# GpSimd subtracts the low parts of a weight tile in two instructions: a decoder trunk in emulated fp32

## The chip, the cores and the metric

The kernel runs on one core of a Trainium2 chip. The metric is the device time of one execution in microseconds (us); the number that counts is the median of the runs. One more execution was recorded by the hardware profiler, and all rows below are from that one.

## The reference

The program is a decoder trunk of two layers over 512 positions of width 1024, in float32, with a batch of one. In each layer the input is normalized, scaled and shifted by vectors that are computed from a condition vector (the "ada" vectors); one wide projection then gives everything that the two branches need:

```python
def hybrid_layer(x, mod, norm_g, w_in, ...):
    shift, scale, gate = jnp.split(mod, 3, axis=-1)
    h = rms_norm(x, norm_g) * (1 + scale[:, None]) + shift[:, None]
    a_qkv, a_z, m_cq, m_ckv, m_kr, m_z, merge = jnp.split(h @ w_in, SPLIT_IDX, axis=-1)
    y_a = dilated_mixer(a_qkv, rel_bias) * jax.nn.silu(a_z)
    y_m = mla_mixer(m_cq, m_ckv, m_kr, q_norm_g, w_uq, kv_norm_g, w_ukv, cos, sin) * jax.nn.silu(m_z)
    g_a, g_m = jnp.split(jax.nn.sigmoid(merge), 2, axis=-1)
    merged = g_a * (y_a @ w_out_a) + g_m * (y_m @ w_out_b)
    return x + gate[:, None] * (merged @ w_o)
```

Branch A is attention over dilated windows, with 3 groups of 8 heads and a bias by relative position; branch B is latent attention with 16 heads and a rotary part. A last normalization follows layer two.

## The kernel before

**Numbers in two parts.** Products are made in a format with a shorter mantissa (fp32r), and each operand is kept as a high part, its value rounded to that format, and a low part, the value less the high part. A product is the sum of three: high by high, low by high, high by low. `split` (line 195) makes the two parts. The high part is a copy on ACT (line 203) or a cast on DVE or POOL (line 205); the low part is one subtraction (line 206), on POOL unless `lo` names DVE. A table, `ENG`, gives for each use the engine of the high and of the low part in turn. POOL is the engine called GpSimd as well.

**Weights.** `wload` (line 231) brings a tile of weights of 1024 inputs by 128 outputs: `load_w` issues its DMA on SP's queue into a `stage` tile (line 224; two buffers), `wpair` takes a high tile `wh` and a low tile `wl` (three buffers each), and `split` fills them. In such a tile the 1024 inputs lie as 8 groups of 128 partitions, so the tile is 128 partitions by 8 x 128 values, 128x1024. The DMA that fills a stage tile again waits for its last reader, the subtraction. `proj` (line 248) then runs over the 8 groups: for each group k it issues three matmuls (line 166), `wh[k]` by the high part of the normalized input (`hTh`), `wl[k]` by the same, and `wh[k]` by the low part (`hTl`). The result lies in a PSUM bank; there are two banks `pj`, three `s`, two `t` and one `o`.

**Stages.** In each layer the projections come in blocks between attention steps: queries and keys of a set of heads (`a_qk`), values (`a_v`), SiLU gates (`zgate`, line 604, whose tile is evacuated at lines 609 and 610), merge gates (`merge_gate`), the latents of branch B (`m_latents`, whose second evacuation is line 952), then 16 heads of branch B (`m_head`), the output projections and the norm. An attention of branch A (`a_attn`) scales its weights `p` by factors of 128x8 values (lines 821 to 844 make them, line 854 scales, partly on DVE, partly on POOL, partly on ACT), transposes them (line 861), splits them into `pth` (line 211) and `ptl` (line 864), and multiplies them by the values `v` into the bank `o`. In layer 0 the ada vectors of later use are accumulated on DVE between these steps (line 286, after a first step on ACT at line 277; their weights are loaded into `lat` tiles at line 272, the sums added to their biases at line 306), the tables of position bias are written to memory and read back as `bvec` and `btile` (lines 529, 537, 541), and the angles of the rotary part are reduced on DVE in a chain of some 25 steps (lines 553 to 576).

**The order.** The program says what depends on what. In which order each engine and each DMA queue does its instructions is decided when the program is built: a scheduler with a simulated timeline (`schedule_with_timeline_sim=True`, line 1362) takes at each point what its estimates of duration say will be ready. An engine then does its list strictly in that order and waits wherever an operand isn't there. So when an instruction changes its count or its estimated length, other engines' lists can change as well.

## Time and profile before

| | us |
|---|---|
| median of 3 runs | 1435.63 |
| fastest and slowest of them | 1433.96, 1441.8 |
| the profiled execution, its own time | 1440.56 |
| its span in the trace | 1438.8 |
| PE busy | 1352.0 |
| DVE busy | 917.5 |
| ACT busy | 704.7 |
| POOL busy | 575.4 |

PE is the matrix engine, PEld its loading of weights beside it, DVE the vector engine, ACT the scalar engine, POOL GpSimd, SP the engine whose queue issues all DMAs. Line numbers are those of the kernel before. The trace gives each instruction's start and duration, and for idle time ahead of it what ended that idle time. The granted clock is the share of PE's full clock in a stretch: 1.00 is the higher of its two levels (2.4 GHz), 0.50 the lower (1.2 GHz).

### The profile page before, as it was taken

The page shows a single profiled execution, that of the slowest core. Times are in us where ns is not written, and L with a number is a line of the kernel's source. Part 1 is how long each engine was busy: PE and PEld are TensorE (multiplying, and loading weights), DVE is VectorE, ACT ScalarE, POOL GpSimd, SP SyncE. Part 2 cuts the span into 40 slices and gives each one's busy share as a digit, 9 for nine tenths or more (in the row PEclk, how much of TensorE's full clock was granted, in tenths as well). Part 3 has the DMA queues.
Part 4 walks back from the last instruction along what each step waited for, and adds up shares of the span by engine and source line. Part 5 has one row for each costly group of instructions (what it writes and reads, how often), then busy time and mean ns, then how long its engine had stood idle before and what let it go on. Part 6 is the DMA issues. An engine that isn't in the chain of part 4 may idle for free.

```text
span 1438.8 us, 21364 instructions
## 1 busy us (share of the span) xinstructions
PE 1352.0 (94%) x7351; PEld 1163.1 (81%) x7351; DVE 917.5 (64%) x2123; ACT 704.7 (49%) x1913; POOL 575.4 (40%) x423
## 2 busy tenths in 40 slices
PE   7989997999999999999989999999999898999997
PEld 6788776798887778888888988789888777888876
DVE  7736758845756767654799346634575586766563
ACT  4424663236566778721034266523655687862102
POOL 2423434334553333355444234533455333344530
PEclk7999998999999999999999999999999999999999
DMA  9776423233244323465753332233324332445641
GB/s 334 236 228 190 148 71 98 85 88 85 70 132 124 93 81 107 122 192 162 209 157 124 112 88 74 81 89 89 83 73 133 110 92 81 111 145 170 185 130 59
DMA packets 236676, 181.47 MB, mean 126 GB/s; under 512 B 16410, under 2 KB 204224, under 8 KB 236568
## 3 DMA queue, kind: packets, MB, share of 16 engines
q1 hardware_dynamic: 236568, 180.11, 42.3%
q8 instruction: 58, 0.95, 0.3%
q14 instruction: 50, 0.41, 0.1%
HBM read 150.60 MB, written 23.17 MB: 121 GB/s over the span
## 4 chain that ended last, share of the span: by engine, by line
PE 64%; DVE 15%; DMA 7%; ACT 5%; issue 5%; POOL 3%; SPq 1%; DVEq 0%; POOLq 0%; ACTq 0%
PE pj L166 38%; PE s L166 19%; PE o L166 4%; PE t L861 3%; DMA stage<-in_w_o 2%; POOL wl L206 2%; DMA lat<-in_w_ada 1%; DVE lat L286 1%; DMA stage<-in_w_in 1%; ACT mn L807 1%; DMA v<-in_w_ada 1%; DVE p L792 1%; DVE ptl L864 1%; DVE wh L205 1%; ACT p L798 1%
## 5 line engine op out<-in xcount | busy, mean ns | idle before, releaser
L206 POOL TENSOR_TENSOR wl<-stage,wh 128x1024 fp32r<-128x1024 f32 (+1 forms) x134 | 316.1, 2360 | 429.3 <-ACT wh L203 230.0
L166 PE MATMUL pj<-hTh,wh 128*128 128x512 f32 (+1 forms) x720 | 286.2, 398 | 22.4 <-DVE wh L205 5.7
L166 PE MATMUL pj<-hTl,wh 128*128 128x512 f32 (+1 forms) x720 | 281.2, 392 | 0.0
L166 PE MATMUL pj<-hTh,wl 128*128 128x512 f32 (+1 forms) x704 | 275.3, 391 | 0.0
L166 PEld LDWEIGHTS pj<-hTh,wh 128*128 128x128 f32 x720 | 138.3, 192 | 52.1 <-issue 14.1
L166 PEld LDWEIGHTS pj<-hTl,wh 128*128 128x128 f32 x720 | 137.0, 191 | 26.6 <-ACT hTl L377 0.7
L203 ACT ACTIVATE wh<-stage 128x1024 fp32r<-128x1024 f32 (+1 forms) x84 | 85.1, 1014 | 142.7 <-PE s L166 71.4
L166 PEld LDWEIGHTS pj<-hTh,wl 128*128 128x128 f32 x704 | 134.1, 191 | 23.4
L864 DVE TENSOR_TENSOR ptl<-t,pth 128x512 fp32r<-128x512 f32 (+2 forms) x160 | 96.4, 617 | 35.3 <-ACT pth L211 34.3
L211 ACT ACTIVATE pth<-t 128x512 fp32r<-128x512 f32 (+2 forms) x160 | 81.8, 537 | 65.4 <-PE t L861 63.5
L166 PE MATMUL s<-kb,qh 128*128 128x256 f32 (+3 forms) x384 | 86.4, 320 | 8.4 <-DVE x L792 3.3
L166 PE MATMUL o<-pth,v 128*64 128x128 f32 (+3 forms) x496 | 91.2, 260 | 3.0 <-DVE yy L915 1.7
L166 PE MATMUL o<-ptl,v 128*64 128x128 f32 (+2 forms) x320 | 79.9, 282 | 7.8 <-DVE ptl L864 7.7
L861 PE MATMUL t<-eye_r,p 128*128 128x128 f32 x560 | 83.9, 280 | 1.7 <-POOL p L854 1.6
L205 DVE CAST wh<-stage 128x1024 fp32r<-128x1024 f32 (+1 forms) x77 | 57.9, 753 | 40.6 <-PE s L166 16.0
L166 PEld LDWEIGHTS s<-kb,qh 128*128 128x128 f32 x384 | 66.5, 191 | 21.3 <-ACT qh L211 4.6
L1093 DVE CUSTOM_DVE_ANT_0 p<-s,cs 128x512 f32<-128x512 f32 (+3 forms) x128 | 58.6, 484 | 30.9 <-PE s L166 30.4
L166 PEld LDWEIGHTS o<-pth,v 128*64 128x64 f32 (+1 forms) x496 | 65.5, 155 | 9.0 <-ACT pth L211 3.1
L861 PEld LDWEIGHTS t<-eye_r,p 128*128 128x128 f32 x560 | 65.6, 143 | 6.7 <-POOL p L854 2.0
L166 PE MATMUL s<-hTh,wh 128*128 128x512 f32 (+1 forms) x168 | 65.8, 392 | 2.3 <-DVE x L792 1.2
L166 PE MATMUL s<-hTh,wl 128*128 128x512 f32 (+1 forms) x168 | 65.5, 390 | 0.0
L166 PEld LDWEIGHTS o<-ptl,v 128*128 128x128 f32 (+1 forms) x320 | 52.4, 164 | 16.1 <-DVE ptl L864 11.8
(713 smaller groups left out, 3302.1 us busy)
## 6 DMA issues: line engine op xcount, KB each, us to landing
stage<-in_w_in SPq DMA_DIRECT2D x118, 512.0 KB
lat<-in_w_ada SPq DMA_DIRECT2D x64, 256.0 KB
v<-in_w_ada SPq DMA_DIRECT2D x32, 256.0 KB
stage<-in_w_in SPq DMA_DIRECT2D x32, 256.0 KB
gd<-gt SPq DMA_DIRECT2D x32, 256.0 KB
stage<-in_w_out_b SPq DMA_DIRECT2D x16, 512.0 KB
stage<-in_w_o SPq DMA_DIRECT2D x16, 512.0 KB
p<-yd SPq DMA_DIRECT2D x24, 256.0 KB
```

The lines of the kernel that those rows point to most:

```text
L166: T.matmul(o, l, r, start=start, stop=stop, skip_group_check=True)
L203: A.activation(dst_h, src, AF.Copy)
L205: hi.tensor_copy(dst_h, src)
L206: (lo or G).tensor_tensor(dst_l, src, f32(dst_h), ALU.subtract)
L211: A.activation(dst, src, AF.Copy)
L286: V.scalar_tensor_tensor(acc, st, cact[:, k:k + 1], side if k == ne + np_ else acc, ALU.mult, ALU.add)
L792: V.tensor_tensor_reduce(pt[e][:, sl], o[:, c0:c0 + 128], bts[e][:, 128 + 128 * g:256 + 128 * g], 1.0, -3e38, ALU.add, ALU.max, x12[:, e, ...
L798: A.activation(pt[e][:, sl], pt[e][:, sl], AF.Exp, bias=m12[:, g - 1, e, p:p + 1], scale=SA, accum_out=l12[:, g - 1, e, p:p + 1])
L807: (A.copy if c == "A" else (G if c == "G" else V).tensor_copy)(dst[32 * p:32 * p + 32, :, qb], src[32 * qb:32 * qb + 32, :, p])
L861: T.transpose(tp[:, 128 * b:128 * b + 128], s, eye)
L864: V.tensor_tensor(lo[:, :n], tp[:, :n], f32(h[:, :n]), ALU.subtract)
L1093: V.tensor_tensor_reduce(pt, o, mask[:, 512 - n:512], 1.0, -3e38, ALU.add, ALU.max, m[:, qb:qb + 1])
```

## The change

In `split`, if the low part is POOL's, and the tile has three dimensions with more than one group of inputs and 1024 values in a partition, POOL does the subtraction in two instructions, one for the first four groups of inputs and one for the last four:

```diff
--- before.py
+++ after.py
@@ -203,6 +203,12 @@
             A.activation(dst_h, src, AF.Copy)
         else:
             hi.tensor_copy(dst_h, src)
+        if lo is None or lo is G:
+            n = dst_l.shape[1]
+            if len(dst_l.shape) == 3 and n > 1 and n * dst_l.shape[2] == 1024:
+                for i in (0, n // 2):
+                    G.tensor_tensor(dst_l[:, i:i + n // 2], src[:, i:i + n // 2], f32(dst_h[:, i:i + n // 2]), ALU.subtract)
+                return
         (lo or G).tensor_tensor(dst_l, src, f32(dst_h), ALU.subtract)
 
     def hi_copy(dst, src, use):
```

That is so for 118 of the 126 subtractions of 128x1024 that POOL has; the other eight, the values of `a_v`, lie in four dimensions and stay whole. Nothing else is written differently. Behind line 207 the line numbers of the changed kernel are 6 higher.

The lists of the engines differ in places. The matmuls of PE are 6958 rows before, and 6622 of them stand in the same order in both; of 2062 rows of DVE 1965 do, of 1172 of ACT 1103, of 628 of SP 594. The differences lie in the first 100 us of layer 0, in layer 0 from the second attention of branch A to the latents, and at the end of both layers (the last heads and the merge gates). In the rows below a name has two numbers, of which the second differs between the two programs without meaning.

PE, layer 0, where the projection of keys (`s_478`) ends and the two tiles of a SiLU gate begin (`pj_489` with `wh_487` and `wl_488`; `pj_494` with `wh_492` and `wl_493`), before:

```order
L861 MATMUL t_422_2047<-eye_r_69,p_390_1859 128x128
L861 MATMUL t_422_2047<-eye_r_69,p_391_1860 128x128 x2
L166 MATMUL s_478_2395<-hTh_55_224,wl_477_2392 128x512
L166 MATMUL s_478_2395<-hTl_56_225,wh_476_2391 128x512
L166 MATMUL pj_489_2469<-hTh_41_210,wh_487_2465 128x512
L166 MATMUL pj_494_2503<-hTh_41_210,wh_492_2499 128x512
L166 MATMUL o_418_2029<-pth_420_2039,v_173_774 128x256
L166 MATMUL o_418_2029<-ptl_421_2040,v_173_774 128x256
L166 MATMUL o_418_2029<-pth_420_2039,v_175_802 128x256
L166 MATMUL o_418_2029<-ptl_421_2040,v_175_802 128x256
```

and now:

```order
L166 MATMUL s_478_2414<-hTh_55_224,wh_476_2409 128x512
L166 MATMUL s_478_2414<-hTh_55_224,wl_477_2410 128x512
L166 MATMUL s_478_2414<-hTl_56_225,wh_476_2409 128x512
L166 MATMUL pj_489_2489<-hTh_41_210,wh_487_2484 128x512
L166 MATMUL pj_494_2524<-hTh_41_210,wh_492_2519 128x512
L166 MATMUL pj_489_2489<-hTh_41_210,wl_488_2485 128x512
L166 MATMUL pj_489_2489<-hTl_42_211,wh_487_2484 128x512
L166 MATMUL pj_489_2489<-hTh_43_212,wh_487_2484 128x512
L166 MATMUL pj_489_2489<-hTh_43_212,wl_488_2485 128x512
L166 MATMUL pj_489_2489<-hTl_44_213,wh_487_2484 128x512
```

The seven transposes (`t_419`, `t_422`) ahead of the end of `s_478` have left, and the first products of the attention (`o_418` with `pth_420` and `ptl_421`) no longer follow the first matmuls of `pj_489` and `pj_494`: nearly all 48 matmuls of the two gate tiles come first, then the transposes, then a matmul of the next tile and `o_418`.

DVE, the same place, around its cast of `wh_492` (line 205), before:

```order
L213 CAST kb_117_453<-s_468_2325 64x4x128
L286 SCALAR_TENSOR_TENSOR lat_369_1818<-lat_374_1831,cact_75,lat_369_1818 128x512
L854 TENSOR_SCALAR p_398_1901<-p_398_1901,f12_417_2026 128x128 x3
L854 TENSOR_SCALAR p_399_1902<-p_399_1902,f12_417_2026 128x128
L428 SCALAR_TENSOR_TENSOR Ac_115_451<-Ac_115_451,vec_76 128x2
L854 TENSOR_SCALAR p_399_1902<-p_399_1902,f12_417_2026 128x128 x2
L667 TENSOR_TENSOR ql_474_2386<-pj_472_2360,qh_473_2385 128x512
L659 TENSOR_TENSOR kb_118_456<-s_468_2325,kb_117_453 64x4x128
L205 CAST wh_492_2499<-stage_491_2497 128x1024
L286 SCALAR_TENSOR_TENSOR lat_369_1818<-lat_375_1834,cact_75,lat_369_1818 128x512
```

and now:

```order
L840 TENSOR_TENSOR L_413_2013<-L_413_2013 128x8
L292 SCALAR_TENSOR_TENSOR lat_369_1831<-lat_374_1844,cact_75,lat_369_1831 128x512
L673 TENSOR_TENSOR ql_474_2404<-pj_472_2378,qh_473_2403 128x512
L665 TENSOR_TENSOR kb_118_459<-s_468_2342,kb_117_456 64x4x128
L841 RECIPROCAL L_413_2013<-L_413_2013 128x8
L205 CAST wh_492_2519<-stage_491_2517 128x1024
L312 TENSOR_TENSOR Bc_116_455<-ada_322_1564,vec_76 128x2
L312 TENSOR_TENSOR Ac_115_454<-ada_322_1564,vec_76 128x2
L292 SCALAR_TENSOR_TENSOR lat_369_1831<-lat_375_1847,cact_75,lat_369_1831 128x512
L843 TENSOR_TENSOR fn_414_2018<-en_412_2009,L_413_2013 128x8
L847 TENSOR_TENSOR f0_416_2037<-en_412_2009,L_413_2013 128x8
L434 SCALAR_TENSOR_TENSOR Ac_115_454<-Ac_115_454,vec_76 128x2
```

The scalings of `p` (line 854, now 860) stand behind the cast, as does the making of the factors `fn` and `f0`; the accumulations of an ada vector (`lat_369`), the evacuations of keys (`kb_118`) and the query's low part (`ql_474`) stand ahead of it as they did.

SP's queue, in the first 100 us of layer 0, where the position bias is written (`bvec`, `btile`) and weights of `a_v` are loaded (`stage_169` to `stage_187`), and two ada weights (`lat_208`, `lat_209`), before:

```order
L224 DMA stage_166_737<-in_w_in 128x4x256
L224 DMA stage_169_743<-in_w_in 128x4x256
L732 DMA stage_184_865<-in_w_in 128x2x256 x2
L529 DMA bvec_437<-gt_149_683 24x512
L732 DMA stage_187_896<-in_w_in 128x2x256 x2
L529 DMA bvec_437<-gt_152_691 24x384
L537 DMA btile_438<-bvec_437 8x32x256 x4
L541 DMA btile_438<-bvec_437 1024x1x128 x2
L272 DMA lat_208_1025<-in_w_ada 128x512
L272 DMA lat_209_1028<-in_w_ada 128x512
```

and now:

```order
L230 DMA stage_166_741<-in_w_in 128x4x256
L535 DMA bvec_440<-gt_149_687 24x512
L543 DMA btile_441<-bvec_440 8x32x256 x4
L230 DMA stage_169_748<-in_w_in 128x4x256
L738 DMA stage_184_870<-in_w_in 128x2x256
L535 DMA bvec_440<-gt_152_695 24x384
L738 DMA stage_184_870<-in_w_in 128x2x256
L547 DMA btile_441<-bvec_440 1024x1x128 x2
L278 DMA lat_208_1030<-in_w_ada 128x512
L738 DMA stage_187_901<-in_w_in 128x2x256 x2
L278 DMA lat_209_1033<-in_w_ada 128x512
```

The first write to `bvec` and the four to `btile` (line 537, now 543) stand ahead of `stage_169` and `stage_184`, and `lat_208` ahead of `stage_187`.

## Rows read from the trace of the kernel before

**Rows 1.** The page of the profiled execution: its line of busy times by engine, and from the chain of work that ended last the shares by engine and by line.

```profile
PE 1352.0 (94%) x7351; PEld 1163.1 (81%) x7351; DVE 917.5 (64%) x2123; ACT 704.7 (49%) x1913; POOL 575.4 (40%) x423
...
PE 64%; DVE 15%; DMA 7%; ACT 5%; issue 5%; POOL 3%; SPq 1%; DVEq 0%; POOLq 0%; ACTq 0%
PE pj L166 38%; PE s L166 19%; PE o L166 4%; PE t L861 3%; DMA stage<-in_w_o 2%; POOL wl L206 2%; DMA lat<-in_w_ada 1%; DVE lat L286 1%; DMA stage<-in_w_in 1%; ACT mn L807 1%; DMA v<-in_w_ada 1%; DVE p L792 1%; DVE ptl L864 1%; DVE wh L205 1%; ACT p L798 1%
```

**Rows 2.** Groups of POOL instructions by line and form (busy us, mean ns of one | idle time of POOL before them and what ended it): the weight subtraction at full size, another subtraction of half the size on the same line, and the eight weight subtractions that were of half the size already.

```profile
L206 POOL TENSOR_TENSOR wl<-stage,wh 128x1024 fp32r<-128x1024 f32 x126 | 305.8, 2428 | 414.8 <-ACT wh L203 215.6 <-DVE wh L205 133.3 <-issue 23.0
...
L206 POOL TENSOR_TENSOR pl<-p,ph 128x512 fp32r<-128x512 f32 x20 | 25.4, 1288 | 20.0 <-ACT ph L203 17.9 <-issue 1.9
...
L206 POOL TENSOR_TENSOR wl<-stage,wh 128x512 fp32r<-128x512 f32 x8 | 10.3, 1290 | 14.5 <-ACT wh L203 14.5
```

**Rows 3.** Waits of PE's weight loads by what ended them (us in total, times, longest us): the only row of the answer that names a weight subtraction of POOL.

```profile
PEld s L166 <- POOL wl L206: 0.6, 1, 0.6
```

**Rows 4.** The chain that ended last, in order of time (start us, us, what): the first and the last of the nine pieces that are a weight subtraction of POOL, and the load behind the first.

```profile
414.23 2.38 POOL wl L206
...
416.62 4.24 DMA stage<-in_w_in
...
1370.96 2.73 POOL wl L206
```

**Rows 5.** Waits of PE's matmuls by what ended them (us in total, times, longest us).

```profile
PE o L166 <- DVE ptl L864: 7.7, 12, 3.3
PE pj L166 <- DVE v L707: 6.6, 3, 4.9
PE pj L166 <- DVE wh L205: 5.7, 1, 5.7
```

**Rows 6.** Busy time by stretch of the span (stretch, its length, then for PE, PEld, DVE, ACT and POOL the busy us and the count of instructions, the granted clock of PE as a share of full speed, the DMA share, GB/s).

```profile
92.00:98.00 6.00, 6.00 (x16) 4.82 (x16) 3.31 (x5) 1.19 (x2) 2.36 (x1) 0.54 0.95 321
220.00:300.00 80.00, 67.83 (x370) 57.12 (x369) 61.50 (x97) 26.36 (x56) 33.66 (x27) 0.89 0.32 88
226.00:232.00 6.00, 0.45 (x2) 0.01 (x1) 5.88 (x13) 2.37 (x6) 5.43 (x6) 0.88 0.19 43
232.00:242.00 10.00, 6.26 (x36) 5.47 (x37) 9.53 (x14) 1.82 (x3) 2.73 (x1) 0.56 0.41 105
282.00:290.00 8.00, 7.52 (x24) 6.11 (x25) 3.76 (x7) 5.49 (x9) 0.00 (x0) 0.59 0.10 24
555.00:625.00 70.00, 67.37 (x367) 57.02 (x366) 49.56 (x118) 48.54 (x127) 25.20 (x17) 1.00 0.49 147
900.00:980.00 80.00, 77.94 (x452) 66.43 (x451) 40.40 (x84) 32.02 (x89) 37.37 (x31) 0.98 0.30 85
1235.00:1305.00 70.00, 68.06 (x370) 57.48 (x370) 48.53 (x116) 48.27 (x126) 24.43 (x16) 1.00 0.47 143
```

**Rows 7.** Timeline of PE (start us, us, instruction, in brackets the idle time before it and what ended it): two matmuls 0.23 us apart before the stop, the two that end it, the one after the next long stop, and the one that ends the stop at 91.65.

```profile
225.82 0.40 PE L166 MATMUL s<-hTl,wh 128*128 128x512 f32 x1
226.05 0.40 PE L166 MATMUL pj<-hTh,wh 128*128 128x512 f32 x1
232.12 0.77 PE L166 MATMUL pj<-hTh,wh 128*128 128x512 f32 x1 [5.67 <-DVE wh L205]
...
236.44 0.58 PE L166 MATMUL o<-ptl,v 128*128 128x256 f32 x1 [3.33 <-DVE ptl L864]
...
282.48 0.77 PE L166 MATMUL pj<-hTh,wh 128*128 128x512 f32 x1 [2.88 <-DVE lat L952]
...
91.65 0.81 PE L166 MATMUL pj<-wh,hTh 128*128 128x512 f32 x1 [4.93 <-DVE v L707]
```

**Rows 8.** Busy time of the scalings of line 854 alone in one stretch (columns as in the group above on stretches).

```profile
221.00:230.00 9.00, 4.11 (x12) 5.96 (x8) 1.00 0.55 146
```

**Rows 9.** Timeline of DVE around these stops.

```profile
216.67 2.38 DVE L832 TENSOR_TENSOR L<-l,en 128x8 f32<-128x8 f32 x1
...
230.21 1.77 DVE L205 CAST wh<-stage 128x1024 fp32r<-128x1024 f32 x1
...
232.56 2.30 DVE L306 TENSOR_TENSOR Bc<-ada,vec 128x2 f32<-128x2 f32 x1
...
281.59 0.74 DVE L952 SCALAR_TENSOR_TENSOR lat<-pj,vec,lat 128x512 fp32r<-128x512 f32 x1
```

**Rows 10.** Timeline of POOL in the same stretch.

```profile
216.59 2.43 POOL L206 TENSOR_TENSOR wl<-stage,wh 128x1024 fp32r<-128x1024 f32 x1 [0.48 <-ACT en L830]
...
232.11 2.73 POOL L206 TENSOR_TENSOR wl<-stage,wh 128x1024 fp32r<-128x1024 f32 x1 [0.68 <-issue]
```

**Rows 11.** The chain that ended last, from 76 us on (SPq is the queue of DMA issues on SP).

```profile
76.66 5.18 SPq L541
...
81.89 7.84 DMA lat<-in_w_ada
...
89.75 0.73 ACT lat L277
...
91.18 0.43 DVE v L707
```

## The prediction

> **What bounds the kernel now.** I began with the page's line of busy times and the chain that ended last. PE is busy 1352.0 of 1438.8 us, POOL 575.4, and the chain is PE for 64% and POOL for 3% [rows 1]: only about 87 us of the span are idle PE, and POOL has room. Then the groups of POOL by form: 126 weight subtractions of 128x1024 take 2428 ns each, and both forms of half that size on the same line take 1288 to 1290 ns [rows 2]. Then I asked who waits for them. PE's weight loads waited for a POOL weight subtraction once, for 0.6 us [rows 3]; PE's long waits are for DVE: 5.7 us for one cast of a high part, 7.7 for low parts of attention weights, 6.6 for low parts of V [rows 5]. In the chain a POOL subtraction stands nine times, between 414.23 and 1370.96 us, and there it holds a stage tile: behind the first, the next weight load of 4.24 us begins [rows 4]. Last I looked at where PE loses its time, by stretches. From 220 to 300 us PE is busy 67.83 of 80 us at a granted clock of 0.89; the stretch 680 us later, where layer 1 does the same stages, has 77.94 of 80 at 0.98 [rows 6]. So the largest loss lies at one place of layer 0, and DVE is what is full there: 5.88 of 6 us and 9.53 of 10.
>
> **The direct effect of the halves.** Two halves take 2 x 1.290 = 2.580 us where one took 2.428, so 0.152 us more. Of the 126 subtractions 118 are cut, which is 118 x 0.152 = 18 us more of POOL; POOL's 863 us of idle time cover it. A low part's first half is there 1.14 us sooner, its last half 0.15 us later. The sooner half is worth 0 to 0.6 us, since only 0.6 us of PE's waiting is for such a tile [rows 3]; I take 0, as PE comes to the first low block only after other work. The later end counts where the subtraction is in the chain: 9 x 0.152 = **+1.4 us**. If a DMA behind it were not waiting for the stage tile, this would be 0.
>
> **What the new order does.** The order of each engine is decided from a simulated timeline, so the longer POOL work shifts other instructions. I compared the orders: most of each list is kept, and three places are rewritten.
>
> First place, 220 to 300 us. PE stops at the first matmul of the second SiLU gate tile (wh_492) for 5.67 us, and then for 3.33 us at the first product with a ptl tile [rows 7]. DVE made the cast at 230.21, behind the scalings of line 854, which took it 4.11 us [rows 8, 9]. In the new order the cast stands ahead of all those scalings and of some small steps (about 1.5 us, an estimate from some ten instructions of 0.15 us), and POOL's subtractions for both gate tiles stand ahead of POOL's scalings. An 8-element DVE step that began at 216.67 beside a POOL subtraction lasted 2.38 us, until that subtraction ended [rows 9, 10]; with a half there it can be held 1.3 us at most, 1.1 less. So the cast begins 4.1 + 1.1 + 0.5 to 1.5 = 5.7 to 6.7 us sooner, at 223.5 to 224.5, and ends at 224.2 to 226.3, by whether it takes 0.7 or 1.77. PE needs it at 226.05, or 0.7 sooner, since seven transposes have left their place ahead of it. The stop of 5.67 becomes 0 to 0.9; I take 0.4. Ahead of the first ptl product PE now has 47 more matmuls of the two gate tiles at 0.227 each, 10.7 us. DVE has 14 to 16 us to do between the cast and that ptl (estimate: the 4.11 of scalings, the 3.7 that lay between the two before, and five to six us of evacuations and casts now ahead of it). So 3 to 5 us of a stop remain; I take 3.5 for the 3.33 of before. DVE stays the fuller engine, and the work that hides the gate tiles is not new work, only placed sooner.
>
> The third stop of this stretch, 2.88 us at 282.48, waits for line 952, which DVE did at 281.59 at the end of the long chain that makes the rope's angles [rows 7, 9]. The new order puts line 952 in the middle of that chain, but the chain begins later, since two attention pieces now come ahead. By the instructions in between I get stops of 0.5 and 2.5 where there was one of 2.88: nothing won.
>
> Each stop also costs clock. After the stops PE had 0.56 of its clock from 232 to 242 and 0.59 from 282 to 290, and did 6.26 and 7.52 us of work in them [rows 6]: 0.44 x 6.26 = 2.8 and 0.41 x 7.52 = 3.1 us lost, one of the two clock levels being half the other. I expect about the same loss again behind two or three short stops. The sum of the stretch: 5.67 + 3.33 + 2.88 = 11.9 before, 0.4 + 3.5 + 3.0 = 6.9 after, and the clock between 0 and 3 better: **-6.5 us**. Its bounds: all idle time gone (12.2) with both losses of clock (5.9) is -18; with nothing gained and two more slow stretches of 3 it is +6.
>
> Second place, the start of layer 0. PE stops for 4.93 us until 91.65 [rows 7]. The chain there: SP is held 5.18 us at line 541, then a load of 7.84 us, ACT's line 277 at 89.75, DVE's line 707 at 91.18 [rows 11]. In the new order the bias writes of lines 529 and 537 stand ahead of two weight loads, and one of the two later loads stands behind; line 541 is held for less. I estimate the load 3 to 6 us sooner, so the stop at 0 to 2, and up to 0.46 x 6 = 2.8 us of clock that PE lost from 92 to 98 [rows 6]. DMA moved 321 GB/s then at 0.95 of its time, so a part is given back to the next loads. I take **-3.0**, with bounds 0 and -7.7.
>
> Third place, the ends of both layers (head pieces and merge gates, 555 to 625 and 1235 to 1305 us). PE is busy 67.37 and 68.06 of 70 there at full clock [rows 6]: 4.6 us could be won at most, and a new order can open stops. I take **+1.0**, bounds -3 and +6.
>
> Elsewhere DVE steps that are held by a POOL subtraction are held shorter, as one of two elements that took 2.30 us beside a subtraction [rows 9, 10]; most of them lie off the chain: **-1.0**, bounds 0 and -5. What the row shows is stated as a rule by the Trainium skill, SBUF — State Buffer (Who interferes with whom): DVE and GpSimd share a pair of ports that one of them holds for its whole instruction while the other is blocked. By that rule alone, the cut would let DVE in halfway each time, and this term would be nearer to its far bound.
>
> The sum: 1.4 - 6.5 - 3.0 + 1.0 - 1.0 = -8.1, so 1440.56 becomes 1432.5. The median of the runs is 1435.63, 4.93 below the profiled execution; the same change puts it at **1427.5 us**.
>
> **Rivals.** *Only the halves act.* The stops at the first place move but keep their size, because DVE has the same work to do (15.4 us busy of the 16 from 226 to 242 [rows 6]); the second place gives back what it wins. Then +1.4 and at most -3 stay: about 1435. For it: DVE is full, and no instruction of DVE is removed. Against: 4.1 us of work is moved behind the cast that ends the longest stop.
>
> *DVE is freed by more than the order.* If the holds of DVE by POOL are halved wherever they stand in the chain, both long stops vanish and the clock stays up: -12 at the first place, -6 at the second, -1 elsewhere, +1.4: about 1418. For it: the DVE steps that began at 216.67 and 232.56 and the POOL subtraction beside each end together [rows 9, 10]. Against: the second half can follow the first at once, and hold DVE again. This is what the rule of the page named above would make of the time.
>
> *Slower.* The long stops turn into more stops. At the first place wh_492, the first ptl, and the two tiles of line 952 each stop PE; if the cast ends after 228 us and each stop is 2.5 to 3 us with 2.9 us of slow clock behind it, the place costs 4 x 5.7 = 22.8 in place of 11.9 + 5.9 = 17.8: +5. With +1.4 and a few us at the ends of the layers it gives about 1444. It decides from a cast that ends after 228.
>
> **How the numbers follow.** About 0.5% (7.2 us) is what a measurement here can tell from no change: faster is below 1428.4, slower above 1442.8. Chances: the forecast (1422 to 1433) 0.46, only the halves 0.25, DVE freed 0.14, slower 0.15. Of the forecast's some 0.30 lies below 1428.4 and 0.16 above; with the freed DVE and a little of the second that makes 0.46 faster; 0.41 same; 0.13 slower. The range 1414 to 1442 leaves out a part of the freest case and most of the slower one.
>
> **What would show it.** Right: POOL near 593 us; 118 pairs of 1.29; the matmul of wh_492 without a long stop and one of about 3.5 us at the first ptl; 220 to 300 us with PE busy 72 or more; the stop near 90 us under 2. Wrong: a cast of wh_492 after 228; new stops at the ends of the layers; pairs that take well over 2.6 us; PE waiting for a POOL weight tile.

## The result, and the profile after

| | before | after |
|---|---|---|
| median of the runs taken side by side, us | 1438.72 (4 runs, 1433.96 to 1441.93) | 1414.65 (4 runs, 1409.67 to 1415.47) |
| the profiled execution, its span, us | 1438.8 | 1407.6 |

The ratio is 0.9838, with a 95% interval of 0.9811 to 0.9865: 1.6% faster. The forecast of 1427.5 against 1435.63 was a ratio of 0.9943. The time lies inside the range, but the gain is nearly three times the forecast's.

The page of the kernel after, its busy times and the chain that ended last:

```profile
PE 1341.5 (95%) x7351; PEld 1156.2 (82%) x7351; DVE 903.9 (64%) x2123; ACT 703.3 (50%) x1913; POOL 598.4 (43%) x541
...
PE 70%; DVE 14%; ACT 5%; DMA 5%; issue 3%; POOL 1%; SPq 1%; DVEq 0%; ACTq 0%; POOLq 0%
```

Against [rows 1] the span fell by 31.2 us: PE's busy time by 10.5 and its idle time, span less busy, by 20.7 (86.8 to 66.1). That is more than the 24.1 us between the medians: the profiled execution of after is the fastest of its four (1409.67 us), that of before was slower than its median (1440.56). PE does the same 7351 matmuls, so less busy time means a higher clock. POOL grew by 23.0 us, and DVE, with the same 2123 instructions, fell by 13.6.

Groups of POOL by form, after (as [rows 2]):

```profile
L210 POOL TENSOR_TENSOR wl<-stage,wh 128x512 fp32r<-128x512 f32 x236 | 308.6, 1330 | 332.8 <-ACT wh L203 159.7 <-DVE wh L205 118.9 <-issue 31.4
L212 POOL TENSOR_TENSOR wl<-stage,wh 128x1024 fp32r<-128x1024 f32 x8 | 20.4, 2549 | 50.7 <-ACT wh L203 50.7
```

The 118 subtractions are 236 halves of 1330 ns. Next, stretches of PE: first before, then after, columns as in [rows 6] but of PE alone.

```profile
0.00:70.00 70.00, 60.27 (x256) 0.83 0.87 293
70.00:110.00 40.00, 35.07 (x186) 0.91 0.67 211
205.00:300.00 95.00, 82.83 (x456) 0.91 0.32 91
620.00:960.00 340.00, 328.49 (x1847) 0.98 0.43 126
960.00:1300.00 340.00, 326.76 (x1814) 1.00 0.37 103
```

```profile
0.00:70.00 70.00, 60.49 (x270) 0.88 0.91 304
70.00:110.00 40.00, 38.08 (x209) 1.00 0.73 221
205.00:300.00 95.00, 90.11 (x496) 1.00 0.38 104
620.00:960.00 340.00, 332.78 (x1923) 0.99 0.42 123
960.00:1300.00 340.00, 327.27 (x1773) 1.00 0.39 112
```

Read each row for two losses: its length less PE busy, and the busy time by which the clock fell short. In the 95 us around the gate tiles 12.2 us idle became 4.9, and a clock of 0.91 over 82.83 us (7.5 us lost) became 1.00. From 70 to 110 us 4.9 idle and 3.2 of clock became 1.9 and none. From 620 to 960, the ends of layer 0 and the first half of layer 1, 11.5 idle became 7.2. From 960 on little changed, and neither did the idle time of the first 70 us; the clock there, 0.83 and 0.88, is no sure sign, since from 0 to 70 us it lay between 0.83 and 0.98 in the experiments below that keep the old order there.

PE's timeline after, the stops that answer to [rows 7]:

```profile
85.68 0.63 PE L166 MATMUL pj<-wh,hTh 128*128 128x512 f32 x1 [1.92 <-DVE v L713]
...
217.83 0.47 PE L166 MATMUL pj<-hTh,wh 128*128 128x512 f32 x1 [2.27 <-DVE Ac L312]
...
230.72 0.50 PE L166 MATMUL pj<-hTh,wh 128*128 128x512 f32 x1 [1.19 <-DVE zs L616]
...
232.81 0.39 PE L166 MATMUL o<-ptl,v 128*128 128x256 f32 x1 [0.72 <-DVE ptl L870]
...
279.59 0.50 PE L166 MATMUL o<-ph,sel_r 64*128 64x512 f32 x1 [0.54 <-ACT ph L203]
```

The 4.93 before the values (V) became 1.92; the 5.67 before wh_492 became 2.27; the 3.33 before the first ptl became 1.19 and 0.72; the 2.88 behind line 952 is gone. The step of DVE named at 217.83 is a neighbour of the real releaser, the cast of wh_492, which DVE did then:

```profile
210.25 1.12 DVE L838 TENSOR_TENSOR L<-l,en 128x8 f32<-128x8 f32 x1
...
211.37 1.79 DVE L292 SCALAR_TENSOR_TENSOR lat<-lat,cact,lat 128x512 f32<-128x512 f32 x1
...
217.04 0.64 DVE L205 CAST wh<-stage 128x1024 fp32r<-128x1024 f32 x1
...
218.40 1.29 DVE L843 TENSOR_TENSOR fn<-en,L 128x8 f32<-128x8 f32 x1
```

and POOL in the same stretch, after:

```profile
210.05 2.55 POOL L210 TENSOR_TENSOR wl<-stage,wh 128x512 fp32r<-128x512 f32 x2
...
217.81 3.12 POOL L210 TENSOR_TENSOR wl<-stage,wh 128x512 fp32r<-128x512 f32 x2 [5.21 <-DVE Ac L312]
```

Line 838 is the step of 2.38 us in [rows 9]. It began 0.2 us into a pair of halves and lasted 1.12, to 211.37; the first half ends at 210.05 + 2.55/2 = 211.33. DVE got through between the two halves. Likewise line 843 began at 218.40 beside the pair that started at 217.81, and ended at 219.69, still inside it. That agrees with the rule of the Trainium skill, SBUF — State Buffer (Who interferes with whom), that GpSimd keeps the shared ports for a whole instruction. The second half holds DVE too: the lat step that followed at 211.37 took 1.79 us, where steps of its kind that nothing holds take 0.74. So a cut lets one step through halfway, and the next can be held again.

### The profile page after: what moved, and what is told of

Its sections match the earlier page's. It is cut to its first block, busy times and chain, and to the rows that moved or that the text cites. A ratio compares the mean times of both kernels' runs of the same rounds, so it can differ in the third digit from the quotient of the medians.

```text
span 1407.6 us, 21528 instructions
## 1 busy us (share of the span) xinstructions
PE 1341.5 (95%) x7351; PEld 1156.2 (82%) x7351; DVE 903.9 (64%) x2123; ACT 703.3 (50%) x1913; POOL 598.4 (43%) x541
## 4 chain that ended last, share of the span: by engine, by line
PE 70%; DVE 14%; ACT 5%; DMA 5%; issue 3%; POOL 1%; SPq 1%; DVEq 0%; ACTq 0%; POOLq 0%
PE pj L166 40%; PE s L166 20%; PE o L166 5%; PE t L867 4%; DMA stage<-in_w_o 2%; DMA lat<-in_w_ada 1%; DVE lat L292 1%; ACT p L804 1%; PE t L166 1%; DVE kb L665 1%; DVE wh L205 1%; DVE wl L212 1%; DMA ql<-pl 1%; DVE ptl L870 1%; DVE p L1099 1%
## 5 line engine op out<-in xcount | busy, mean ns | idle before, releaser
L210 POOL TENSOR_TENSOR wl<-stage,wh 128x512 fp32r<-128x512 f32 x236 | 308.6, 1330 | 332.8 <-ACT wh L203 159.7
L166 PEld LDWEIGHTS pj<-hTl,wh 128*128 128x128 f32 x720 | 135.7, 189 | 26.9 <-issue 1.0
L166 PEld LDWEIGHTS pj<-hTh,wl 128*128 128x128 f32 x704 | 133.9, 190 | 23.5
L205 DVE CAST wh<-stage 128x1024 fp32r<-128x1024 f32 (+1 forms) x77 | 59.4, 773 | 41.3 <-PE s L166 12.9
L166 PE MATMUL s<-hTl,wh 128*128 128x512 f32 (+1 forms) x168 | 64.3, 383 | 0.0
```

Of the source, the lines that this page charges most:

```text
L166: T.matmul(o, l, r, start=start, stop=stop, skip_group_check=True)
L205: hi.tensor_copy(dst_h, src)
L210: G.tensor_tensor(dst_l[:, i:i + n // 2], src[:, i:i + n // 2], f32(dst_h[:, i:i + n // 2]), ALU.subtract)
```

## The experiments

**How an order is held.** In most of these kernels the order of every engine is written into the kernel as a table, and each instruction is tied to the one ahead of it on its engine:

```python
def pinned(nc, tc, halves):
...
        for d in v[at + 1:at + 1 + n]:
            x += d
            for i in mine[x]:
                if prev is not None:
                    tc.add_manual_dep(i, prev.name, mybir_.DependencyInfo(
                        mybir_.DependencyClass.NoSync, mybir_.DependencyReason.DATA), reason="pinned")
                prev = i
```

Only the order is fixed by that; `halves` says how many instructions each of the 118 subtractions has. What the tie itself costs is not measured, since no run ties the uncut kernel to its own order; the trace of e2 has as many semaphore waits (1577) as that of the changed kernel, which has no tie. So the two things that the change does, the cut and the new order, can be had one without the other.

The table has, for each kernel, the ratio to the kernel before on the same chip, the lead (start of PE's n-th matmul less that in the trace of before, for n = 500, 1300, 5000, 7300, which before starts at 123.7, 295.8, 981.6 and 1422.0 us), and PE's idle time in two stretches of the trace. "Old" and "new" are the order of before and of after. In the expectations, "first place" is the start of layer 0; the text here says start and gate place (205 to 300 us).

| kernel | ratio, 95% interval | lead at 500, 1300, 5000, 7300, us | idle 0:110, us | idle 205:300, us; clock |
|---|---|---|---|---|
| before | 1 | 0 | 14.7 | 12.2; 0.91 |
| the change | 0.9838, 0.9811 to 0.9865 | -8.5, -23.1, -26.9, -30.7 | 11.4 | 4.9; 1.00 |
| e1 whole, new | 0.9906, 0.9882 to 0.9929 | -9.0, -19.1, -13.6, -13.7 | 10.8 | 4.6; 0.98 |
| e2 halves, old | 0.9949, 0.9930 to 0.9968 | -0.8, -3.5, -12.5, -11.6 | 14.0 | 11.5; 0.93 |
| e3 halves, new at the start | 0.9902, 0.9882 to 0.9922 | -8.9, -13.5, -19.7, -18.7 | 9.8 | 11.4; 0.93 |
| e4 halves, new at the gate place | 0.9902, 0.9881 to 0.9924 | -1.8, -16.7, -20.2, -19.1 | 14.9 | 3.8; 0.98 |
| e5 halves by outputs, old | 0.9951, 0.9931 to 0.9972 | -3.6, -7.0, -12.5, -12.4 | 15.0 | 11.3; 0.93 |
| e6 quarters, new | 0.9820, 0.9793 to 0.9846 | -5.8, -23.6, -21.7, -21.2 | 11.1 | 4.5; 0.98 |
| e9 quarters, old | 0.9918, 0.9896 to 0.9941 | -0.2, -9.7, -12.5, -10.3 | 15.2 | 9.2; 0.93 |
| e7 as e3, SP old | 0.9955, 0.9933 to 0.9977 | -0.6, -3.4, -6.0, -4.5 | 16.5 | 11.4; 0.93 |
| e8 halves, old, gate tiles first | 0.9991, 0.9973 to 1.0009 | +0.2, 0.0, -3.8, -4.0 | 16.3 | 13.8; 0.95 |
| e12 as e8, ACT too | 0.9965, 0.9950 to 0.9980 | -1.5, -3.8, -9.1, -8.7 | 13.4 | 12.9; 0.96 |
| e13 halves, old, latent sooner | 0.9939, 0.9915 to 0.9963 | -1.3, -4.3, -9.8, -8.2 | 13.9 | 11.8; 0.95 |
| e14 as e4, ACT's copies old | 0.9919, 0.9897 to 0.9941 | -0.8, -11.7, -16.7, -19.0 | 13.5 | 7.0; 0.98 |
| e15 as e4, SP's load old | 0.9885, 0.9862 to 0.9907 | -0.6, -14.5, -18.6, -17.5 | 14.4 | 3.6; 0.98 |
| e16 as e4, PE's run-up old | 0.9883, 0.9859 to 0.9906 | -2.7, -17.3, -21.3, -23.5 | 15.3 | 3.4; 0.98 |
| e17 halves, new at both | 0.9852, 0.9822 to 0.9882 | -9.5, -23.6, -28.8, -26.9 | 11.1 | 3.9; 0.98 |

A lead is of one profiled execution each; where it and the ratio differ by a few us, the ratio counts.

**e1_order_alone and e2_halves_alone: the two parts of the change.** e1 is the kernel before, in the order of after; e2 the kernel after, in the order of before.

```diff
 e1: before
+ORDER = (
...
+)
...
         trunk(tc, *args, out)
+        pinned(nc, tc, 1)
 e2: after
+ORDER = (
...
+)
...
         trunk(tc, *args, out)
+        pinned(nc, tc, 2)
```

> Each weight subtraction is one instruction, as before the change, and all five engines keep the order of the changed kernel. Theory A (the order alone): the ratio to the kernel before is that of the change, 0.984 (about 1415 us), and the stretch from 210 to 290 us loses as little PE time as there. Theory B (the halves themselves: DVE is held for less long, and stage tiles and low parts are ready sooner): the new order alone gives little, 0.995 to 1.005. Theory C (the order, but only with halves beside it): 0.988 to 0.993, with DVE steps of 8 elements that again last about 2.3 us ahead of the cast of wh_492, and PE's stop there 1 to 2 us longer than in the changed kernel (2.27).

> The 118 subtractions are cut in halves, and all five engines keep the order of the kernel before. Theory A: no gain; 1.000 to 1.002, since 0.15 us more stands in the chain nine times; the stops of 5.67 and 3.33 us stay within 0.5 us. Theory B: 0.984 to 0.990, and both stops shrink to under half. Theory C: 0.996 to 0.999: DVE is held about 1.1 us less ahead of the cast that ends the stop of 5.67, which becomes some 4.5.

The order alone gave 0.9906 and the halves alone 0.9949; their product is 0.9855, within the interval of the change. So both act: the order some 13.5 us (0.94% of 1436.6), the halves 7.3 (0.51%). That is not what any one theory said: e1 lies in the band of theory C, but its stop at wh_492 (2.18) is no longer than that of the change, and e2 lies between the bands of B and C. The leads say where. In e1 the order has all of its lead by the 1300th matmul and loses some later; in e2 the halves win 9 us between there and the 5000th, across the border of the layers (5.5 in e5, which follows).

**e5_column_halves: is it the sooner half, or the shorter instruction?** Each of the two instructions takes all eight groups of inputs and half of the outputs. A matmul needs all outputs of a group, so nothing can be used before the second has ended.

```diff
-                for i in (0, n // 2):
-                    G.tensor_tensor(dst_l[:, i:i + n // 2], src[:, i:i + n // 2], f32(dst_h[:, i:i + n // 2]), ALU.subtract)
+                m = dst_l.shape[2]
+                for i in (0, m // 2):
+                    G.tensor_tensor(dst_l[:, :, i:i + m // 2], src[:, :, i:i + m // 2], f32(dst_h[:, :, i:i + m // 2]), ALU.subtract)
```

> The order of the kernel before on all engines, and each of the 118 subtractions in two instructions, but cut by the outputs (the first and the last half of the columns of all groups of inputs) in place of the inputs. So a matmul needs both instructions as it needed the one, and nothing is ready sooner; only the time that POOL is in one instruction is halved. If the halves alone gained (0.995) because DVE is held for less long: 0.995 again (0.993 to 0.997). If they gained because the first low parts are ready 1.1 us sooner: 1.000 to 1.002.

0.9951 beside 0.9949: the gain of the halves is not that a low part can be used sooner, since here none can (the two intervals would hide some 4 us). What is left is that POOL's instruction is shorter.

**e9_quarters_before_order and e6_quarters: shorter still.** Four instructions of 128x256, in the old and in the new order.

```diff
-                for i in (0, n // 2):
-                    G.tensor_tensor(dst_l[:, i:i + n // 2], src[:, i:i + n // 2], f32(dst_h[:, i:i + n // 2]), ALU.subtract)
+                for i in range(0, n, n // 4):
+                    G.tensor_tensor(dst_l[:, i:i + n // 4], src[:, i:i + n // 4], f32(dst_h[:, i:i + n // 4]), ALU.subtract)
```

> Quarters: each subtraction in four instructions of 128 x 256, in the order of before on every engine. Theory 1 (what the halves bring in that order is that GpSimd lets go of VectorE sooner, so a shorter instruction brings a little more): VectorE's held time falls below that of the halves, ratio 0.990 to 0.994. Theory 2 (a shorter hold brings nothing further and GpSimd's work grows by 40 us more): ratio 0.996 or more. In between, neither.

> The order of the changed kernel on all engines, and each of the 118 subtractions in four instructions, two groups of inputs in each. If holding DVE for less long is what the halves bring, there is a little more of it to have: DVE's steps held by a POOL subtraction fall from about 1.2 to about 0.7 us, and the ratio is 0.981 to 0.984. If POOL's extra time (another 0.3 us or so for each tile, 35 us in all) ends up in the waits: 0.986 to 0.990.

The pages' lines of busy time, of e2 (halves), then of e9 (quarters), both in the old order:

```profile
PE 1348.5 (95%) x7351; PEld 1163.9 (82%) x7351; DVE 904.7 (63%) x2123; ACT 704.6 (49%) x1913; POOL 596.6 (42%) x541
```

```profile
PE 1349.3 (94%) x7351; PEld 1163.1 (81%) x7351; DVE 900.6 (63%) x2123; ACT 706.8 (49%) x1913; POOL 638.1 (45%) x777
```

DVE does the same 2123 instructions in the same order in these and before: 917.5 us beside whole subtractions [rows 1], 904.7 beside halves (908.9 in e5), 900.6 beside quarters. What falls is the time that DVE is held: a step with an input in a PSUM bank is as long as before, as the 112 `ptl` steps show, 685 ns in the mean before and in e2. Whether quarters hold less than halves this number doesn't say, since in all the kernels with halves it lies between 899 and 912. POOL pays 21 us for the first cut and 41 more for the second, in time it has. In the old order quarters gave 0.9918, in the band of the theory of the hold; its interval still touches that of the halves. In the stretch where the halves win most, from the 3000th matmul to the 5000th, the two kernels with quarters won only 0.7 and 1.9 us. In the new order quarters (0.9820) and halves (0.9838) can't be told apart.

A place where the hold acts, at the border of the layers, in the trace before (DVE, then POOL, then PE):

```profile
774.92 1.70 DVE L286 SCALAR_TENSOR_TENSOR lat<-lat,cact,lat 128x512 f32<-128x512 f32 x1
...
777.25 0.69 DVE L677 TENSOR_TENSOR ql<-pj,ql 64x512 fp32r<-64x512 f32 x1
777.97 2.12 DVE L286 SCALAR_TENSOR_TENSOR lat<-lat,cact,lat 128x512 f32<-128x512 f32 x1
```

```profile
777.16 2.38 POOL L206 TENSOR_TENSOR wl<-stage,wh 128x1024 fp32r<-128x1024 f32 x1
```

```profile
777.36 0.36 PE L166 MATMUL s<-wh,hTh 128*128 128x256 f32 x1 [1.01 <-DVE ql L667]
...
791.49 0.36 PE L166 MATMUL pj<-wh,hTh 128*128 128x256 f32 x1 [1.77 <-DVE kb L659]
```

The ql step, one of whose inputs is a PSUM bank, ran through the same subtraction in 0.69 us; the lat step, whose inputs are both in SBUF, took 2.12. The same page and section of the Trainium skill makes this difference between one SBUF input and two; the trace agrees.

The same steps of DVE and the stop of PE that is left in e2, with halves and in the same order:

```profile
767.51 0.74 DVE L292 SCALAR_TENSOR_TENSOR lat<-lat,cact,lat 128x512 f32<-128x512 f32 x1
...
769.61 1.01 DVE L292 SCALAR_TENSOR_TENSOR lat<-lat,cact,lat 128x512 f32<-128x512 f32 x1
```

```profile
781.92 0.36 PE L166 MATMUL pj<-wh,hTh 128*128 128x256 f32 x1 [0.58 <-DVE kb L665]
```

The two lat steps took 1.70 + 2.12 = 3.82 us beside whole subtractions and 0.74 + 1.01 = 1.75 beside halves, 2.1 less; the two stops of PE behind them fell from 2.78 to 0.58, 2.2 less. (Between the two stops one more lat step is held, for 2.95 and 2.70 us; in e2 that is beside a subtraction of `a_v`, which stays whole.) e1, whole subtractions in the new order, has both stops still (1.01 and 1.76), and in no other kernel with halves is either over 0.5. So here held steps stand ahead of PE, and the cut is what shortens the stops.

**e3_halves_order_first_place and e7_first_place_old_sp: the start of layer 0.** Both are e2 with a piece of the table from after:

```diff
 e3: ORDER, first 262 rows of PE, 130 of DVE, 65 of ACT, 25 of POOL, 100 of SP
-    as before
+    as after
 e7: ORDER, first 262 rows of PE, 130 of DVE, 65 of ACT, 25 of POOL (SP as before)
-    as before
+    as after
```

> Halves; the order of the changed kernel only from the start to about 110 us of layer 0 (position bias, first values), and that of the kernel before from there on. Theory A: the first place is worth its part, some 8 us by the two traces at the stop near 91 us and what follows to 145: 0.994. Theory B: as the halves alone. If the lead of the first place is given back at the next wait for a load: 0.999 to 1.001.

> As e3 (halves, the new order only in the first place, ratio 0.990), but SP's queue keeps the order of the kernel before there too. If the order of the loads and bias writes on SP is what ends the stop of 4.93 us near 91 us, this gives that back: a stop of 4 to 5 us there, 0.994 to 0.996. If the order of PE, DVE and ACT is what counts: 0.990.

The new order at the start takes 0.9949 to 0.9902, 6.8 us, a larger gain than the 0.994 expected; without SP's part it gives 0.9955, nothing. PE's stop at the values in e7, longer than the 4 to 5 us expected:

```profile
91.69 0.81 PE L166 MATMUL pj<-wh,hTh 128*128 128x512 f32 x1 [7.87 <-DVE v L713]
```

SP's queue tells why. Of e7, and then of after, the chain that ended last (as [rows 11]):

```profile
76.16 6.42 SPq L547
...
82.62 6.55 DMA lat<-in_w_ada
```

```profile
71.32 0.69 SPq L547
...
72.05 1.30 SPq L547
...
73.40 4.32 SPq L278
...
78.77 5.68 DMA lat<-in_w_ada
```

In the old order SP sits at line 547 (541 before) for 6.42 us while the ada load stands behind it; in the new one the two DMAs of that line take it 2.0 us. SP still stands for 4.32 us, but at the issue of the first ada load (line 278), from 73.40 on; that issue came at 82.62 in e7. The load that ends the chain now is the next one, and it lands at 84.45 instead of 89.73 [rows 11]. So SP's part is needed; whether it would do by itself no run shows.

**e4_halves_order_gate_place: the gate place.** The new order from about 165 to 310 us only.

```diff
 e4: ORDER, rows 660 to 1500 of PE, 265 to 450 of DVE, 200 to 310 of ACT, 45 to 105 of POOL, 100 to 190 of SP
-    as before
+    as after
```

> Halves; the order of the changed kernel only from about 165 to 310 us of layer 0 (the second attention of branch A, the gate tiles, the latents), that of the kernel before elsewhere. Theory A: worth some 12 us by the two traces: 0.991 to 0.992. Theory B: as the halves alone. With the first place (0.994) it should give 0.985 to 0.986; what is left to 0.984 is then the rest of the order.

It takes 0.9949 to 0.9902, 6.8 us as well, a little more than the 0.991 to 0.992 expected. Idle time falls from 11.5 to 3.8 us, the clock rises from 0.93 to 0.98; e1 shows the same without halves (4.6; 0.98). So the order does most of it here.

**e8_gate_first and e12_gate_first_act: the step that the forecast rested on.** In the old order, with halves, PE takes the 48 gate matmuls first, DVE's twelve scalings stand behind the cast of wh_492, and POOL's two gate tiles ahead of its scalings. In e12 ACT's three evacuations (kb_117, qh_473, lat_323) stand ahead of its sixteen copies into fp as well, and DVE's fn and f0 behind the cast.

```diff
 e8 and e12: PE
-L861 t_419, t_422 x7; L166 s_478 x2; pj_489 x1; pj_494 x1; o_418
+L166 s_478 x2; pj_489 x1; pj_494 x1; pj_489 x23; pj_494 x23; L861 t_419, t_422 x7; o_418
 e8 and e12: DVE
-L854 p x12; L205 wh_492
+L205 wh_492; L854 p x12
 e12 alone: ACT
-L807 fp_415 x16; L211 kb_117; L211 qh_473; L300 lat_323
+L211 kb_117; L211 qh_473; L300 lat_323; L807 fp_415 x16
```

> Halves, the order of the kernel before, and of the second place only the step that the prediction speaks of: all matmuls of the two gate tiles ahead of the transposes and first products of the attention on PE, the twelve scalings of DVE behind the cast of wh_492, POOL's cast and subtractions for the gate tiles ahead of its scalings. SP and ACT keep their order. If this step is the worth of that place (12 us in e4's trace, 3 of them from the halves): 0.990 to 0.992, with stops of under 1 and 1 to 3 us for 4.06 and 4.52 with halves alone. If the load of stage_491, which SP issues no sooner than before, holds the cast: a stop of 2 to 4 us, 0.993 to 0.995.

> Halves, the order of before on every engine, but at the gate place: TensorE takes the 48 gate matmuls first, VectorE's twelve scalings stand behind the cast of wh_492, GpSimd's two gate tiles stand ahead of their scalings (all as in the run with the gate matmuls alone), and in addition ScalarE takes the three evacuations kb_117, qh_473 and lat_323 ahead of the sixteen copies into fp, and VectorE takes fn, f0 and their scalings right behind the cast, f12 and its scalings later. Theory 1 (ScalarE's sixteen copies, which stood ahead of kb_117, kept the cast of wh_492 back): the cast runs near 217 to 222 instead of behind 224, the stop of 3.84 at 226.56 shrinks to 2.5 or less, and the ratio falls from 0.9991 to 0.992 to 0.996. Theory 2 (the gate matmuls first cost what they bring, since the products that filled the time of the pattern tiles are then missing later): the stop near 226 shrinks, but as much comes back by 290, and the ratio stays at 0.997 or more.

e8 gave 0.9991, outside both expectations: the step by itself gains nothing, and takes the gain of the halves away. ACT and PE in e8:

```profile
218.07 3.28 ACT L813 COPY fp<-fn 32x2 f32<-32x2 f32 x16 [3.35 <-DVE fn L843]
221.37 0.59 ACT L217 ACTIVATE kb<-s 64x512 fp32r<-64x512 f32 x1
```

```profile
226.56 0.47 PE L166 MATMUL pj<-hTh,wh 128*128 128x512 f32 x1 [3.84 <-DVE wh L205]
...
282.52 0.77 PE L166 MATMUL pj<-hTh,wh 128*128 128x512 f32 x1 [4.34 <-DVE lat L958]
```

ACT evacuated kb only behind sixteen small copies; DVE's kb_118 and the cast stand behind that. With ACT mended, e12's cast came at 223.76 in place of 225.72, but PE was there 1.5 us sooner as well, and its stop only shrank from 3.84 to 3.41. The ratio is 0.9965, between the bands of the two theories, so neither is borne out. The stop behind line 958 (952 before) stayed at 4.38 us, where e2 has 2.66. So at least a part of what was won ahead was given back at the end of the rope chain.

**e13_latent_sooner: that last stop by itself.** e2, with lat_514 ahead of the two rope products.

```diff
 DVE
-L306 Bc_116; L306 Ac_115; L952 lat_514
+L952 lat_514; L306 Bc_116; L306 Ac_115
```

> Halves, the order of before on every engine, but for one step of VectorE: the eight-element latent of line 952 (lat_514) runs ahead of the two rope products Bc and Ac instead of behind them. Theory 1 (the stop of 2.7 to 2.9 near 281 is this step's place in VectorE's order): the stop falls under 1.0, and the lead over the kernel before grows by 2 to 3 us between 275 and 295; ratio 0.992 to 0.994, against 0.9949 of the halves alone. Theory 2 (the products behind it are held by the rope instead): a stop of 1.5 or more stays within 10 us of there, and the ratio stays within 0.001 of 0.9949.

PE's timeline in e13:

```profile
285.01 0.39 PE L166 MATMUL pj<-wh,hTh 128*128 128x256 f32 x1 [2.27 <-DVE lat L958]
```

A stop of 2.27 us is left 5 us further on, and 0.9939 can't be told from the halves' 0.9949. Theory 2 is the nearer one.

**e14_gate_old_mn, e15_gate_old_load, e16_gate_old_runup: which engine's piece.** Each is e4 less one piece of one engine's order.

```diff
 e14: ACT
-L217 kh_457; L203 wh_476; L813 mn_410 x16
+L813 mn_410 x16; L217 kh_457; L203 wh_476
 e15: SP
-lat_374; row_321; lat_375; stage_491; ada_322; lat_376
+row_321; lat_374; ada_322; lat_375; lat_376; stage_491
 e16: PE, rows 810 to 916
-    as after
+    as before
```

> Halves; the new order on every engine from 165 to 310 us of layer 0, the order of before elsewhere; but ScalarE takes its sixteen copies into mn (line 813) ahead of the evacuation kh_457 and the cast of wh_476, as before. Theory 1 (the new order gains because ScalarE serves the projections first, so that the chain of evacuations to the cast of wh_492 starts sooner): the stop at wh_492 grows from about 2 to 4 us or more and the ratio from 0.9902 to 0.993 or more. Theory 2 (this piece carries nothing, since the 3.3 us of copies only change places with 1.6 us of others): 0.989 to 0.992.

> Halves; the new order on every engine from 165 to 310 us of layer 0, the order of before elsewhere; but SP issues the load of stage_491 behind the write row_321 and the read ada_322, as before. Theory 1 (the gain rests on stage_491 being there when VectorE reaches the cast of wh_492): the load is issued 2 to 4 us later, the stop at wh_492 grows by as much, ratio 0.992 or more. Theory 2 (the load has time to spare): the stop is as in the whole order of the gate place, ratio 0.989 to 0.992.

> Halves; the new order on every engine from 165 to 310 us of layer 0, the order of before elsewhere; but TensorE keeps its order of before in the some hundred matmuls ahead of the keys' projection s_478 (among them the ends of s_456, s_468 and pj_472). Theory 1 (the new order gains because these projections end sooner, so that ScalarE and VectorE get their evacuations sooner): the cast of wh_492 comes later and the ratio is 0.993 or more. Theory 2 (it is the order behind s_478 that gains): 0.989 to 0.992.

e15 (0.9885, the same stop of 2.27 at wh_492) and e16 (0.9883, the cast at 221.10) are no worse than e4: theory 2 for both, neither SP's load nor PE's run-up carries the gain. In e14 the cast of wh_492 began at 228.42 in place of e4's 223.33, and PE waited for it 5.44 us in place of 2.26:

```profile
229.21 0.76 PE L166 MATMUL pj<-hTh,wh 128*128 128x512 f32 x1 [5.44 <-DVE Ac L312]
```

The idle time of the stretch is 7.0 in place of 3.8. So the mechanism of theory 1 is there, but the ratio, 0.9919, lies in the band of theory 2, and its interval covers e4's 0.9902; e15 and e16, timed beside it, are 0.0035 lower. ACT's piece is worth 0 to 5 us, then, and the larger part of the idle time saved (11.5 to 7.0) stays without it.

**e17_two_places: is there anything else?** Halves, the new order at the start and at the gate place, the old one elsewhere.

```diff
 e17: ORDER, the rows of e3 and the rows of e4
-    as before
+    as after
```

> Halves; the new order at the start of layer 0 and from 165 to 310 us, on every engine; the order of before everywhere else, the ends of both layers included. Theory 1 (the two places and the halves are all of the change): 0.982 to 0.986, a lead over the kernel before of 25 us or more at the end. Theory 2 (the new order of the layers' ends has a part of the gain of its own): 0.9865 or more, with the lead missing from 700 us on and at the last 100 us.

0.9852, a lead of 26.9 us: theory 1. The two places and the halves are the change, within what can be measured; the new order at the ends of the layers adds at most a few us.

## Why the prediction was right and wrong

The sign, the two places, and the mechanism at the start were right; the sizes were not. By the runs, of 1438 us: halves 7.3, order at the start 6.8, order at the gate place 6.8, together 20.9 of the 23.3 that 1.62% is. Each is uncertain by 3 or 4 us, and the rest lies within that.

- **The halves, put at +1.4 for the chain and -1.0 "elsewhere": -7.3 (-4.6 to -10.1).** This is the step that failed. The text saw the hold (2.38 and 2.30 us, [rows 9, 10]) and then said of the held steps that "most of them lie off the chain". No row bore that out. DVE is 15% of the chain [rows 1] and was busy 12.8 us less in e2 and 8.6 in e5. The kernels with halves gained 2 to 8 us of lead between the 3000th matmul (617 us) and the 5000th, where e1, with whole subtractions, lost 3; at 777 and 791 us two stops of PE, 2.8 us in all, stood behind held steps, and 0.58 of it was left in e2. The far bound of that term, -5, was near the truth, and so was the sentence on what the rule of ports alone would make of it. That a second half follows the first at once spoke against it; 210.25 in the profile after shows that DVE gets in between, and 211.37 that the second half does hold the next step.
- **The +1.4 in the chain** isn't seen in the time. POOL's share of the chain fell from 3% to 1%, but by the order: it is 1% in e1 and still 3% in e2.
- **The direct gain of a sooner half, taken as 0:** right by e5, within some 4 us.
- **The start of layer 0, put at -3.0 (0 to -7.7): -6.8 by e3 against e2.** The mechanism, SP's line 541 and the load behind it, is borne out by e7. The stop came out at 1.92, inside the 0 to 2 expected. What was mis-sized is what was thought to be given back: behind that stop PE was busy for all 12 us from 86 to 98 at a clock of 1.00, where 92 to 98 had 0.54 [rows 6], and the lead was not lost later.
- **The gate place, put at -6.5:** by the runs -6.8, so the size of the order's part was right, but by luck: it was put together wrongly. Expected were 6.9 us of stops where 11.9 stood; there were 2.27 + 1.19 + 0.72 + 0.54 = 4.7. The clock was to gain 0 to 3 us; the trace of after has 1.00 over the whole stretch, where 7.5 us were lost. So the profile shows 7.3 + 7.5 = 14.8 us there, more than the ratios of e3 and e4 give to it; some 1.8 of it is this execution's good fortune, since e1, e4 and e17 have 0.98; how much of that is the order's, with halves, the runs don't settle closer than 6.8 give or take 4. The stop at wh_492 was to be 0.4 and was 2.27: the cast came at 217.04, but PE was there at 215.56. In e16, where PE's run-up is the old one, the stop is 0.50 and the time no worse.
- **The step it rested on, gate tiles ahead of scalings:** not enough. e8 does it alone and gains nothing. The stop in e14 shows that ACT's order has a say in when the cast can come; e12, which mends one piece of it, shortened the stop by 0.4 us only. The forecast read PE's, DVE's, POOL's and SP's lists and never weighed ACT's. Which pieces of the new order together suffice isn't settled: single pieces (e14 to e16) could be taken out with little loss, and the step on which the forecast rested could not be put in by itself with gain.
- **The ends of the layers, put at +1.0:** e17 leaves them out and is not told apart from the change.
- **The rivals.** "DVE is freed by more than the order" (1418, chance 0.14) came nearest. Its mechanism is the halves' part, but it gave the loss at the two places to the holds; e1 shows that the order alone ends most of it. So its nearness is in part luck. "Only the halves act" (1435, chance 0.25) is answered by e1, "slower" by a cast that came at 217.04.

## What to carry to other kernels

A long GpSimd instruction can hold a VectorE step with two SBUF operands that begins beside it until it ends. In this kernel cutting it cost GpSimd little; count the held VectorE steps over the whole trace and ask which of them stand ahead of PE, before calling them off the chain. Where a scheduler makes the order, a small edit has two effects, and fixing the order in a table is the way to have them apart; read all five engines' lists, since in e14 sixteen small copies on ScalarE, put back ahead of two other steps, made TensorE's stop 3 us longer.

## What the runs showed of the hardware that was not expected

The same stop had different consequences for the clock in different kernels' executions. First the stretch behind the stop of 2.27 us of after, which ended at 217.83; then the same stop in e17 and the stretch behind it (columns as in [rows 6]):

```profile
218.00:221.00 3.00, 3.00 (x14) 2.47 (x14) 3.00 (x5) 1.20 (x7) 3.00 (x3) 1.00 0.61 163
```

```profile
217.31 0.77 PE L166 MATMUL pj<-hTh,wh 128*128 128x512 f32 x1 [2.25 <-DVE Ac L312]
...
217.00:220.00 3.00, 2.69 (x6) 2.15 (x7) 3.00 (x7) 0.80 (x5) 2.70 (x2) 0.50 0.67 173
```

In after the clock stayed at 2.4 GHz; in e17 it was at 1.2 GHz, and likewise behind this stop in e1 (2.18 us), e4 (2.26) and e15 (2.27). The forecast counted a loss behind each short stop; for this one that was right in those four, and the change's own profile escaped it.

A cut of 128x1024 into two cost POOL 2 x 1.330 - 2.428 = 0.23 us each, where other instructions of that size led to expect 0.15; quarters of 0.770 cost 0.42 more.
